# Moving operands of the Up and Down products: runs of 4 everywhere, weights 64 bytes off, another first matmul

## The chip, the cores and the metric

The kernel runs on one core of a Trainium2 chip. The metric is the device time of one execution in microseconds (us); the time before is the median of three executions, 1084.04 us (1083.44 to 1085.48). The engines have short names: PE is TensorE's matmul, PEld its loading of weights (of the stationary operand), DVE is VectorE, ACT is ScalarE, POOL is GpSimd, SP is SyncE, which issues the DMAs here.

## The reference

One layer of a hybrid decoder on 256 tokens with 2048 features, in float32. A combined input projection feeds two groups of heads, a state-space scan (SSD) and sparse attention; an output projection and a squared-ReLU MLP follow. By work it is nearly all four matrix products:

```python
h = rmsnorm(x, g_mix) @ w_in            # 256 x 2048 @ 2048 x 5728
...                                     # conv, SSD scan, index, top-k, attention
x = x + jnp.concatenate([y_ssd, y_att], axis=-1) @ w_out   # 2048 x 2048
u = rmsnorm(x, g_mlp) @ w_up            # 2048 x 8192
return x + jnp.square(jax.nn.relu(u)) @ w_down             # 8192 x 2048
```

## The kernel before

Precision comes from splitting. Each float32 operand is written as a rounded part hi and a rest lo (type float32r), and a product is hi·hi + hi·lo + lo·hi, three matmuls. `operands` (L119) brings in one piece of the weights by DMA into a tile `raw`, ScalarE casts it to hi (L135), VectorE subtracts to get lo (L136). Both lie in one tile `w2` of a ring of five, first hi, then lo, behind `shift` floats at the tile's start. Pieces are fetched ahead as buffers come free.

There are three forms of product. TensorE's instructions stand in the order in which the program is written; other tasks (attention, scan) are slipped in between by `step()`.

- `product` (L159) has tokens on partitions. The stationary operand is a 128 x 128 block of tokens (`hx`, `yah`/`yal`, `ysh`/`ysl`, `uh`/`ul`), the moving one a row of up to 512 weights. For each of 16 blocks kt along the contraction and each half b of the tokens it issues L173 (hi·hi), L175 (lo of the tokens, hi of the weights) and L176 (hi of the tokens, lo of the weights). It serves the input blocks k, m0 (304 columns), m1 (304), q0, q1, z0, z1, the output projection w_out (four blocks) and Down (four quarters q of four blocks, 384 matmuls in a quarter).
- `product_t` (L211) has features on partitions: the stationary operand is a block of weights, the moving one 256 tokens of `hx` (L224). It serves the input blocks qi and xbc.
- `product_w` (L231) is like it for the Up product, with hi and lo of the tokens side by side in `x2x`: a wide matmul of 512 columns (hi of the weights), then a narrow one of 256 (lo of the weights), both on L245. There are four quarters of 256 such pairs.

The order of the MLP is Up 0, Up 1, Down 0, Up 2, Down 1, Up 3, Down 2, Down 3.

The moving operand and the output are not streamed column by column from first to last. `walk` (L154) reorders them: with runs of 4 and steps of 16 it first takes columns 0 to 3, 16 to 19, 32 to 35 and so on to the end, then 4 to 7, 20 to 23, and so on, four sweeps in all. "Runs of 8" means 8 columns of every 32. `product_t` and the last Down block (`tail`) are not walked.

In the built program `hx`, `x2x`, `yah`, `yal`, `ysh`, `ysl`, `uh`, `ul` and all five `w2` buffers begin 96 bytes past a multiple of 128 in each partition, and slices within them are multiples of 128 bytes apart. So the distance between moving and stationary operand, modulo 128 bytes, is the shift: in `product` 8 floats (32 bytes) for the input blocks, w_out and Down 0 and 2, 24 floats (96 bytes) for Down 1 and the first three blocks of Down 3, 48 floats (192, that is 64 modulo 128) for the tail; in `product_t` 16 floats (64 bytes); in `product_w` 32 floats (128) for quarters 0 and 1 and none for quarters 2 and 3.

Where TensorE did something else just before a product, its first matmul is split in two: the list `other` collects what was issued, `interrupted` (L142) reads it. In `product` and `product_w` the first piece has 32 columns.

Of the kernel before, what the change touches and what calls it, by code (L numbers as in the profile page):

```python
# [18 lines left out]
T = 256  # L19
# [10 lines left out]
WB = 5  # L30
RB = 4

SPARE = 64
SHIFT = 16

QUADS, EIGHTS = (4, 16), (8, 32)
FIRST = 32
UP = [(QUADS, QUADS, 32), (QUADS, QUADS, 32), (EIGHTS, QUADS, 0), (EIGHTS, QUADS, 0)]  # L40
DOWN = [8, 24, 8, 24]


Z0, XBC0, DT0, Q0, K0, V0, QI0, KI0, WI0, END = (
# [31 lines left out]
def hymba_kernel(ctx: ExitStack, tc: tile.TileContext, xn, xt, w_in, w_out, w_up, w_down, vcol, vrow, out):  # L76
    nc = tc.nc
# [27 lines left out]
    def step():  # L105
        for t in list(tasks):
            if isinstance(t[1], int) and t[1] > 0:
                t[1] -= 1
            elif not isinstance(t[1], str) or t[1] in done:
                advance(t)  # L110
# [9 lines left out]
    def operands(src, n, load=None, shift=0, parts=2):  # L120

        pitch = (n + 63) // 64 * 64
        with tc.high_priority(offset=HP):
            raw = wts.tile([P, parts, pitch], F32, name="raw", tag="raw", bufs=RB)
            both = wts.tile([P, 2 * parts * pitch + SPARE], F32R, name="w2", tag="w2", bufs=WB)
            hi, lo = (both[:, shift + i * parts * pitch:shift + (i + 1) * parts * pitch]
                      .rearrange("p (k c) -> p k c", k=parts)[:, :, :n] for i in range(2))
            src = src.rearrange("p (k c) -> p k c", k=parts)
            step = parts if load is None else 1
            for i in range(0, parts, step):  # L130
                s = slice(i, i + step)
                nc.sync.dma_start(raw[:, s, :n], src[:, s])
                if load is not None:
                    load()
                nc.scalar.copy(hi[:, s], raw[:, s, :n])  # L135
                nc.vector.tensor_tensor(lo[:, s], raw[:, s, :n], hi[:, s].bitcast(F32), op=OP.subtract)  # L136
        return hi, lo
# [3 lines left out]
    def interrupted(kind):  # L141

        yes = any(o != kind for o in other)
        other.clear()
        return yes

    def mp(name):
        other.append(name)
        return ps.tile([P, 512], F32, name=name, tag="mid")

    def accumulator():
        return ps.tile([P, 512], F32, name="acc", tag="acc")

    def walk(a, way):  # L154

        run, step = way
        return a.rearrange("p (c k i) -> p k c i", k=step // run, i=run)

    def product(src, n, left, load=None, tail=None, shift=8):  # L159


        acc = [accumulator(), accumulator()]
        last = KT if tail is None else KT - 4

        def part(kt, out, b, wh, wl):
            s = slice(b * P, (b + 1) * P)
            ah, al = left(kt)
            free = tail is not None
            go = (lambda a: a) if free else (lambda a: walk(a, QUADS))

            at = [0, FIRST, n] if kt + b == 0 and interrupted("product") and not free else [0, out.shape[-1]]
            for i, j in zip(at, at[1:]):
                nc.tensor.matmul(go(out[:, i:j]), ah[:, s], go(wh[:, i:j]), start=(kt + i == 0), stop=False,  # L173
                                 skip_group_check=True)
            nc.tensor.matmul(go(out), al[:, s], go(wh), start=False, stop=False, skip_group_check=True)  # L175
            nc.tensor.matmul(go(out), ah[:, s], go(wl), start=False, stop=(kt == KT - 1), skip_group_check=True)  # L176

        kept = []
        halves = [slice(0, n // 2), slice(n // 2, n)]
        if tail is not None:  # L180
            acc.append(mp("acc_t"))
        for kt in range(KT):
            if kt % 2 == 0:
                hi, lo = operands(src[kt // 2], n, load, shift)
            wh, wl = hi[:, kt % 2], lo[:, kt % 2]
            if tail is None:
                for b in range(NB):
                    part(kt, acc[b][:, :n], b, wh, wl)
            elif kt < last:
                for c in halves if kt else [slice(0, n)]:  # L190
                    part(kt, acc[0][:, c], 0, wh[:, c], wl[:, c])
                for i, c in enumerate(halves):
                    part(kt, acc[1 + i][:, c], 1, wh[:, c], wl[:, c])
            else:
                kept.append((kt, wh, wl))
            step()
        if tail is not None:
            for kt, wh, wl in kept:
                for c in halves:
                    part(kt, acc[0][:, c], 0, wh[:, c], wl[:, c])  # L200
            tail(0, slice(0, n), acc[0])
            for i, c in enumerate(halves):
                for kt, wh, wl in kept:
                    part(kt, acc[1 + i][:, c], 1, wh[:, c], wl[:, c])
                tail(1, c, acc[1 + i][:, c])
        other.append("product")
        return acc

    def product_t(src, right):

        acc = accumulator().rearrange("p (c t) -> p c t", c=2)  # L211
        for i in range(4):
            hi, lo = operands(src[i], 1024, shift=SHIFT, parts=1)
            c = i % 2
# [13 lines left out]
        other.append("narrow")  # L228
        return acc

    def product_w(src, right, wide, narrow, shift):  # L231

        acc = [accumulator(), accumulator()]
        for i in range(4):
            hi, lo = operands(src[i], 1024, shift=shift, parts=1)
            out = acc[i % 2]
            for k in range(8):
                x = right(8 * (i // 2) + k)
                s = slice(k * P, (k + 1) * P)
                todo = [(hi, 0, 2 * T, wide), (lo, 0, T, narrow)]  # L240

                if interrupted("wide"):
                    todo[:1] = [(hi, 0, FIRST, wide), (hi, FIRST, 2 * T - FIRST, wide)]
                for j, (w, at, n, way) in enumerate(todo):
                    nc.tensor.matmul(walk(out[:, at:at + n], way), w[:, 0, s], walk(x[:, at:at + n], way),  # L245
                                     start=(i < 2 and k + j == 0), stop=(i >= 2 and k == 7 and j == len(todo) - 1),
                                     skip_group_check=True)
                if k % 4 == 3:
                    step()
        other.append("wide")  # L250
        return acc
# [47 lines left out]
    for name, cols in IN_BLOCKS:  # L299
        n = sum(b - a for a, b in cols)  # L300
# [3 lines left out]
    def in_block(name, load=None):  # L304
        o, n = in_off[name]
        src = w_in[o:o + n * D].rearrange("(g p c) -> g p c", g=8, p=P)
        return product(src, n, h_left, load)
# [434 lines left out]
    def run():  # L742
# [58 lines left out]
        for j in range(4):  # L801
            spawn(residual(j, product(w_out[j], 512, y_left)), f"res{j}")
# [4 lines left out]
    def x2(kt):  # L807
        if kt >= KT - 4:
            need("res3")
        return box[0][:, kt, :]  # L810

    first = product_w(w_up[0], x2, *UP[0])
    while tasks:
        step()
    sst = keep.tile([P, NB], F32, name="sst")
# [10 lines left out]
    def up(q):  # L826
        uh = mlp.tile([P, KT, T], F32R, name="uh")
        ul = mlp.tile([P, KT, T], F32R, name="ul")
        for j in range(8):
            r = mlp.tile([P, 2, T], F32, name="r")  # L830
            for c, acc in enumerate(first if q + j == 0 else product_w(w_up[8 * q + j], x2, *UP[q])):
                nc.scalar.copy(r[:, c], acc[:, T:])
                nc.vector.tensor_tensor(r[:, c], r[:, c], acc[:, :T], op=OP.add)  # L833
            nc.vector.scalar_tensor_tensor(r, r, 0.0, r, op0=OP.max, op1=OP.mult)
            s = slice(2 * j, 2 * j + 2)
            nc.scalar.copy(uh[:, s, :], r)
            nc.vector.tensor_tensor(ul[:, s, :], r, uh[:, s, :].bitcast(F32), op=OP.subtract)
        return uh, ul

    def down(q, u):  # L840
        for j in range(4):

            def add(b, c, acc):
                c = slice(512 * j + c.start, 512 * j + c.stop)
                nc.vector.scalar_tensor_tensor(xr[:, b, c], acc, rs4[:, b:b + 1], xr[:, b, c], op0=OP.mult, op1=OP.add)  # L845
                if q == 3:
                    nc.sync.dma_start(out[b * P:(b + 1) * P, c], xr[:, b, c])

            end = q == 3 and j == 3
            acc = product(w_down[4 * q + j], 512, lambda kt: (u[0][:, kt, :], u[1][:, kt, :]), tail=add if end else None, shift=48 if end else DOWN[q])  # L850
            for b in range(0 if end else NB):
                add(b, slice(0, 512), acc[b])

    u = [up(0)]
    for q in range(1, 4):
        u.append(up(q))
        down(q - 1, u[q - 1])
    down(3, u[3])


# [50 lines left out]
```

## Time and profile before

| | us |
|---|---|
| median of 3 executions | 1084.04 |
| profiled execution | 1085.21 |
| its span, first to last instruction | 1083.4 |
| TensorE busy | 1077.0 |
| weight loads busy | 946.2 |
| VectorE busy | 681.8 |
| ScalarE busy | 526.8 |

The profile is of one execution. Matmuls overlap in it: each is shown from its start to the end of its way through the array, and the next starts before that. The busy time of an engine counts overlapping time once. A row on a source line gives the shortest, middle and longest duration of its instructions and when the first and the last of them started.

### The profile page before, as it was taken

The page shows a single profiled execution, that of the slowest core. Times are in us where ns is not written, and L with a number is a line of the kernel's source. Part 1 is how long each engine was busy: PE and PEld are TensorE (multiplying, and loading weights), DVE is VectorE, ACT ScalarE, POOL GpSimd, SP SyncE. Part 2 cuts the span into 40 slices and gives each one's busy share as a digit, 9 for nine tenths or more (in the row PEclk, how much of TensorE's full clock was granted, in tenths as well). Part 3 has the DMA queues.
Part 4 walks back from the last instruction along what each step waited for, and adds up shares of the span by engine and source line. Part 5 has one row for each costly group of instructions (what it writes and reads, how often), then busy time and mean ns, then how long its engine had stood idle before and what let it go on. Part 6 is the DMA issues. An engine that isn't in the chain of part 4 may idle for free.

```text
span 1083.4 us, 15687 instructions
## 1 busy us (share of the span) xinstructions
PE 1077.0 (99%) x6086; PEld 946.2 (87%) x6086; DVE 681.8 (63%) x971; ACT 526.8 (49%) x725; POOL 24.4 (2%) x30
## 2 busy tenths in 40 slices
PE   9999999999999999999999999999999999999998
PEld 7999999888888888899888888888888888888888
DVE  6776899677765566666665556665455665555553
ACT  6755565556755454455543334444334444333331
POOL 0020000122000000000000000000000000000000
PEclk9999999999999999999999999999999999999999
DMA  9865446544375555555555555555555555555662
GB/s 303 278 214 176 156 127 199 184 148 136 120 269 179 191 191 198 195 195 196 198 198 194 197 195 193 197 199 188 186 192 194 195 194 195 194 194 195 214 214 77
DMA packets 64762, 207.41 MB, mean 191 GB/s; under 512 B 7216, under 2 KB 13616, under 8 KB 64688
## 3 DMA queue, kind: packets, MB, share of 16 engines
q1 hardware_dynamic: 64544, 206.36, 57.2%
q8 instruction: 48, 0.79, 0.3%
q14 instruction: 26, 0.21, 0.1%
q10 hardware_dynamic: 144, 0.05, 0.0%
HBM read 204.29 MB, written 2.10 MB: 190 GB/s over the span
## 4 chain that ended last, share of the span: by engine, by line
PE 95%; DMA 2%; DVE 2%; issue 1%; ACT 0%; SPq 0%; DVEq 0%; ACTq 0%
PE acc L245 32%; PE acc L173 16%; PE acc L176 16%; PE acc L175 16%; PE acc L224 9%; DMA raw<-in_w_in 2%; DVE w L136 1%; PE ps_y L622 1%; PE ps_sr L706 0%; PE ps_l L660 0%; PE ps_o L685 0%; DMA xT<-in_xt 0%; PE ps_s L512 0%; PE ps_s L513 0%; PE ps_dec L613 0%
## 5 line engine op out<-in xcount | busy, mean ns | idle before, releaser
L136 DVE TENSOR_TENSOR w<-raw,w 128x1024 fp32r<-128x1024 f32 (+3 forms) x400 | 466.5, 1169 | 370.9 <-ACT w L135 370.1
L135 ACT CAST w<-raw 128x1024 fp32r<-128x1024 f32 (+3 forms) x400 | 398.6, 999 | 496.2 <-PE acc L176 249.0
L245 PE MATMUL acc<-x2x,w 128*128 128x512 f32 (+2 forms) x2053 | 344.1, 328 | 0.0
L245 PEld LDWEIGHTS acc<-x2x,w 128*128 128x128 f32 x2053 | 308.2, 188 | 35.2
L173 PE MATMUL acc<-w,uh 128*128 128x512 f32 (+2 forms) x530 | 199.3, 377 | 0.0
L175 PE MATMUL acc<-w,ul 128*128 128x512 f32 (+1 forms) x527 | 199.0, 378 | 0.0
L176 PE MATMUL acc<-w,uh 128*128 128x512 f32 (+1 forms) x527 | 199.0, 378 | 0.0
L173 PEld LDWEIGHTS acc<-w,uh 128*128 128x128 f32 x530 | 99.0, 187 | 19.2
L176 PEld LDWEIGHTS acc<-w,uh 128*128 128x128 f32 x527 | 98.6, 187 | 19.1
L175 PEld LDWEIGHTS acc<-w,ul 128*128 128x128 f32 x527 | 98.6, 187 | 19.1
L224 PE MATMUL acc<-hx,w 128*128 128x256 f32 (+1 forms) x978 | 115.1, 277 | 0.0
L224 PEld LDWEIGHTS acc<-hx,w 128*128 128x128 f32 x978 | 112.8, 188 | 0.0
L173 PE MATMUL acc<-w,hx 128*128 128x512 f32 (+3 forms) x229 | 84.5, 372 | 0.4 <-ACT w L135 0.4
L176 PE MATMUL acc<-w,hx 128*128 128x512 f32 (+1 forms) x224 | 81.2, 362 | 0.1
L175 PE MATMUL acc<-w,hx 128*128 128x512 f32 (+1 forms) x224 | 81.0, 361 | 0.0
L173 PEld LDWEIGHTS acc<-w,hx 128*128 128x128 f32 x229 | 43.0, 189 | 6.9 <-ACT w L135 0.8
L176 PEld LDWEIGHTS acc<-w,hx 128*128 128x128 f32 x224 | 42.1, 188 | 6.9 <-DVE w L136 1.1
L175 PEld LDWEIGHTS acc<-w,hx 128*128 128x128 f32 x224 | 42.3, 189 | 6.4 <-issue 0.7
L845 DVE SCALAR_TENSOR_TENSOR xr<-acc,rs,xr 128x512 f32<-128x512 f32 (+1 forms) x32 | 22.3, 736 | 9.2 <-PE acc L176 9.2
L833 DVE TENSOR_TENSOR r<-r,acc 128x256 f32<-128x256 f32 x64 | 26.6, 416 | 0.0
L173 PE MATMUL acc<-w,yah 128*128 128x512 f32 (+2 forms) x68 | 25.7, 387 | 0.0
L175 PE MATMUL acc<-w,yal 128*128 128x512 f32 x64 | 24.7, 386 | 0.0
(215 smaller groups left out, 691.8 us busy)
## 6 DMA issues: line engine op xcount, KB each, us to landing
raw<-in_w_up SPq DMA_DIRECT2D x128, 512.0 KB, 3.3
raw<-in_w_down SPq DMA_DIRECT2D x128, 512.0 KB, 3.3
raw<-in_w_in SPq DMA_DIRECT2D x72, 512.0 KB, 3.5
raw<-in_w_out SPq DMA_DIRECT2D x32, 512.0 KB, 3.3
raw<-in_w_in SPq DMA_DIRECT2D x16, 256.0 KB, 4.3
raw<-in_w_in SPq DMA_DIRECT2D x16, 152.0 KB, 5.4
raw<-in_w_in SPq DMA_DIRECT2D x8, 304.0 KB, 3.2
xT<-in_xt SPq DMA_DIRECT2D x16, 128.0 KB, 4.4
```

What stands on the lines that cost most here:

```text
L135: nc.scalar.copy(hi[:, s], raw[:, s, :n])
L136: nc.vector.tensor_tensor(lo[:, s], raw[:, s, :n], hi[:, s].bitcast(F32), op=OP.subtract)
L173: nc.tensor.matmul(go(out[:, i:j]), ah[:, s], go(wh[:, i:j]), start=(kt + i == 0), stop=False, skip_group_check=True)
L175: nc.tensor.matmul(go(out), al[:, s], go(wh), start=False, stop=False, skip_group_check=True)
L176: nc.tensor.matmul(go(out), ah[:, s], go(wl), start=False, stop=(kt == KT - 1), skip_group_check=True)
L224: nc.tensor.matmul(acc[:, c, at:at + n], w[:, 0, s], x[:, fr:fr + n], start=(i + k + j == 0), stop=(i >= 2 and k == 7 and j == len(todo) - ...
L245: nc.tensor.matmul(walk(out[:, at:at + n], way), w[:, 0, s], walk(x[:, at:at + n], way), start=(i < 2 and k + j == 0), stop=(i >= 2 and k ...
L622: nc.tensor.matmul(pt[:, 64 * i:64 * i + 64], m[i // 4][:, i % 4, :], xdt[:, c, 64 * h:64 * h + 64], start=True, stop=True)
L833: nc.vector.tensor_tensor(r[:, c], r[:, c], acc[:, :T], op=OP.add)
L845: nc.vector.scalar_tensor_tensor(xr[:, b, c], acc, rs4[:, b:b + 1], xr[:, b, c], op0=OP.mult, op1=OP.add)
```

## The change

Four things change. `product_w` takes runs of 4 and steps of 16 for both matmuls and a shift of 32 floats in all quarters, where quarters 2 and 3 had runs of 8 of 32 in the wide matmul and no shift. `product` shifts its weights by 16 floats (64 bytes) everywhere but in the tail, which stays at 48. The split first matmul of `product` has 320 and 192 columns instead of 32 and 480, and blocks of 304 columns (m1) are not split. `product_w` keeps 32 and 480. All start addresses but the weights' stay as they are.

```diff
-QUADS, EIGHTS = (4, 16), (8, 32)
-FIRST = 32
-UP = [(QUADS, QUADS, 32), (QUADS, QUADS, 32), (EIGHTS, QUADS, 0), (EIGHTS, QUADS, 0)]
-DOWN = [8, 24, 8, 24]
+SHIFT_W = 32
+
+RUN = 4
+STEP = 16
+
+FIRST = 320
+FIRST_W = 32
...
-    def walk(a, way):
-
-        run, step = way
-        return a.rearrange("p (c k i) -> p k c i", k=step // run, i=run)
-
-    def product(src, n, left, load=None, tail=None, shift=8):
+    def walk(a):
+
+        return a.rearrange("p (c k i) -> p k c i", k=STEP // RUN, i=RUN)
+
+    def product(src, n, left, load=None, tail=None):
...
-            go = (lambda a: a) if free else (lambda a: walk(a, QUADS))
-
-            at = [0, FIRST, n] if kt + b == 0 and interrupted("product") and not free else [0, out.shape[-1]]
+            go = (lambda a: a) if free else (lambda a: walk(a))
+
+            at = [0, FIRST, n] if kt + b == 0 and interrupted("product") and n == 512 and not free else [0, out.shape[-1]]
...
-                hi, lo = operands(src[kt // 2], n, load, shift)
+                hi, lo = operands(src[kt // 2], n, load, SHIFT if tail is None else SPARE - SHIFT)
...
-    def product_w(src, right, wide, narrow, shift):
+    def product_w(src, right):
...
-            hi, lo = operands(src[i], 1024, shift=shift, parts=1)
+            hi, lo = operands(src[i], 1024, shift=SHIFT_W, parts=1)
...
-                todo = [(hi, 0, 2 * T, wide), (lo, 0, T, narrow)]
+                todo = [(hi, 0, 2 * T), (lo, 0, T)]

                 if interrupted("wide"):
-                    todo[:1] = [(hi, 0, FIRST, wide), (hi, FIRST, 2 * T - FIRST, wide)]
+                    todo[:1] = [(hi, 0, FIRST_W), (hi, FIRST_W, 2 * T - FIRST_W)]
...
-            acc = product(w_down[4 * q + j], 512, lambda kt: (u[0][:, kt, :], u[1][:, kt, :]), tail=add if end else None, shift=48 if end else DOWN[q])
+            acc = product(w_down[4 * q + j], 512, lambda kt: (u[0][:, kt, :], u[1][:, kt, :]), tail=add if end else None)
```

On TensorE, at the place where Down 0 follows Up 1, stands this before (a row is line, operation, output and operands, shape; 4x2x4 is four sweeps of two runs of 4, thus 32 columns):

```order
L245 MATMUL acc<-x2x,w_5549 128x4x32x4
L245 MATMUL acc<-x2x,w_5549 128x4x16x4
L173 MATMUL acc<-w_5579,uh 128x4x2x4
L173 MATMUL acc<-w_5579,uh 128x4x30x4
L175 MATMUL acc<-w_5579,ul 128x4x32x4
```

And this now, at the same place:

```order
L245 MATMUL acc<-x2x,w_5548 128x4x32x4
L245 MATMUL acc<-x2x,w_5548 128x4x16x4
L173 MATMUL acc<-w_5578,uh 128x4x20x4
L173 MATMUL acc<-w_5578,uh 128x4x12x4
L175 MATMUL acc<-w_5578,ul 128x4x32x4
```

The first L173 grows from 32 to 320 columns and the second shrinks from 480 to 192; nothing else moves. The next place is on TensorE too, where Up 2 follows Down 0. Before (4x16x8 is four sweeps of sixteen runs of 8):

```order
L176 MATMUL acc<-w_6119,uh 128x4x32x4
L245 MATMUL acc<-x2x,w_6143 128x32
L245 MATMUL acc<-x2x,w_6143 128x4x15x8
L245 MATMUL acc<-x2x,w_6143 128x4x16x4
L245 MATMUL acc<-x2x,w_6143 128x4x16x8
L245 MATMUL acc<-x2x,w_6143 128x4x16x4
```

And now:

```order
L176 MATMUL acc<-w_6118,uh 128x4x32x4
L245 MATMUL acc<-x2x,w_6142 128x4x2x4
L245 MATMUL acc<-x2x,w_6142 128x4x30x4
L245 MATMUL acc<-x2x,w_6142 128x4x16x4
L245 MATMUL acc<-x2x,w_6142 128x4x32x4
L245 MATMUL acc<-x2x,w_6142 128x4x16x4
```

The number and the sizes of the instructions stay; the wide ones are walked in runs of 4. The shift of the weights shows in no row, since rows carry no addresses. The whole program has one matmul less, at the start of m1.

## Rows read from the trace of the kernel before

**Rows 1.** The page's engine table and clock by fortieths of the span.
```profile
PE 1077.0 (99%) x6086; PEld 946.2 (87%) x6086; DVE 681.8 (63%) x971; ACT 526.8 (49%) x725; POOL 24.4 (2%) x30
...
PEclk9999999999999999999999999999999999999999
```
**Rows 2.** The page's chain of work that ended last, by engine and line.
```profile
PE 95%; DMA 2%; DVE 2%; issue 1%; ACT 0%; SPq 0%; DVEq 0%; ACTq 0%
PE acc L245 32%; PE acc L173 16%; PE acc L176 16%; PE acc L175 16%; PE acc L224 9%; DMA raw<-in_w_in 2%; DVE w L136 1%; PE ps_y L622 1%; PE ps_sr L706 0%; PE ps_l L660 0%; PE ps_o L685 0%; DMA xT<-in_xt 0%; PE ps_s L512 0%; PE ps_s L513 0%; PE ps_dec L613 0%
```
**Rows 3.** Waits of PE: waited for, us in total, times, longest us.
```profile
PE ps_w L260 <- POOL ones L255: 1.3, 1, 1.3
PE ps_ki L438 <- DVE kd L433: 1.2, 1, 1.2
PE acc L173 <- ACT w L135: 0.4, 1, 0.4
```
**Rows 4.** Windows: length; busy PE, PEld, DVE, ACT, POOL; clock; DMA share, GB/s.
```profile
0.00:27.00 27.00, 25.73 (x108) 21.16 (x109) 18.13 (x40) 18.62 (x39) 1.29 (x10) 1.00 0.92 302
27.00:54.00 27.00, 26.36 (x201) 25.37 (x199) 19.94 (x76) 21.44 (x51) 0.00 (x0) 1.00 0.82 281
...
558.80:645.50 86.70, 86.70 (x389) 72.00 (x387) 45.31 (x43) 34.33 (x34) 0.00 (x0) 1.00 0.58 194
731.50:820.60 89.10, 89.10 (x389) 72.06 (x387) 45.34 (x43) 34.31 (x34) 0.00 (x0) 1.00 0.56 189
```
**Rows 5.** L175, Down 0 to 3: count, duration min/median/max ns, first and last start.
```profile
L175 PE MATMUL acc<-w,ul x128: 380/385/393, 559.2 to 645.0; 128*128 128x512 f32 x128
L175 PE MATMUL acc<-w,ul x128: 380/392/397, 731.9 to 820.1; 128*128 128x512 f32 x128
L175 PE MATMUL acc<-w,ul x128: 380/385/393, 906.9 to 992.8; 128*128 128x512 f32 x128
L175 PE MATMUL acc<-w,ul x96: 383/386/391, 993.4 to 1057.6; 128*128 128x512 f32 x96
```
**Rows 6.** L175 in three stretches: w_out late, w_out middle, m1.
```profile
L175 PE MATMUL acc<-w,ysl x16: 381/381/381, 376.6 to 386.5; 128*128 128x512 f32 x16
L175 PE MATMUL acc<-w,yal x4: 397/397/397, 343.3 to 345.4; 128*128 128x512 f32 x4
L175 PE MATMUL acc<-w,hx x22: 294/294/294, 168.1 to 176.5; 128*128 128x304 f32 x22
```
**Rows 7.** L224 of `product_t`, 81 to 99 us; L175 in Down 3's tail.
```profile
L224 PE MATMUL acc<-hx,w x161: 276/276/276, 80.8 to 98.9; 128*128 128x256 f32 x161
L175 PE MATMUL acc<-w,ul x30: 276/276/276, 1060.9 to 1073.8; 128*128 128x256 f32 x30
```
**Rows 8.** L245 of Up quarters 1, 2 and 3, wide and narrow together.
```profile
L245 PE MATMUL acc<-x2x,w x509: 271/382/382, 473.8 to 558.5; 128*128 128x512 f32 x85, 128*128 128x256 f32 x85
L245 PE MATMUL acc<-x2x,w x508: 272/331/404, 645.8 to 730.9; 128*128 128x256 f32 x85, 128*128 128x512 f32 x85
L245 PE MATMUL acc<-x2x,w x509: 272/380/460, 820.6 to 905.9; 128*128 128x256 f32 x85, 128*128 128x512 f32 x84, 128*128 128x480 f32 x1
```
**Rows 9.** Lines by form, 181 to 297 and 297 to 387 us: busy, mean ns.
```profile
L175 PE MATMUL acc<-w,hx 128*128 128x512 f32 x128 | 49.2, 384 | 0.0
...
L175 PE MATMUL acc<-w,yal 128*128 128x512 f32 x64 | 24.7, 386 | 0.0
...
L175 PE MATMUL acc<-w,ysl 128*128 128x512 f32 x64 | 24.5, 382 | 0.0
```
**Rows 10.** Timeline where Down 0 begins: start us, length us, count; loads, then matmuls.
```profile
558.71 0.30 PEld L173 LDWEIGHTS acc<-w,uh 128*128 128x128 f32 x2
558.93 0.19 PEld L175 LDWEIGHTS acc<-w,ul 128*128 128x128 f32 x1
...
558.82 0.49 PE L173 MATMUL acc<-w,uh 128*128 128x32 f32 x2
559.15 0.38 PE L175 MATMUL acc<-w,ul 128*128 128x512 f32 x1
```

More of the change, by code (lines that the diff above doesn't have):

```diff
@@ L239, in product_w @@
                 s = slice(k * P, (k + 1) * P)
-                todo = [(hi, 0, 2 * T, wide), (lo, 0, T, narrow)]
+                todo = [(hi, 0, 2 * T), (lo, 0, T)]
                 if interrupted("wide"):
-                    todo[:1] = [(hi, 0, FIRST, wide), (hi, FIRST, 2 * T - FIRST, wide)]
-                for j, (w, at, n, way) in enumerate(todo):
-                    nc.tensor.matmul(walk(out[:, at:at + n], way), w[:, 0, s], walk(x[:, at:at + n], way),
+                    todo[:1] = [(hi, 0, FIRST_W), (hi, FIRST_W, 2 * T - FIRST_W)]
+                for j, (w, at, n) in enumerate(todo):
+                    nc.tensor.matmul(walk(out[:, at:at + n]), w[:, 0, s], walk(x[:, at:at + n]),
                                      start=(i < 2 and k + j == 0), stop=(i >= 2 and k == 7 and j == len(todo) - 1),
@@ L810, in x2 @@
         return box[0][:, kt, :]
-    first = product_w(w_up[0], x2, *UP[0])
+    first = product_w(w_up[0], x2)
     while tasks:
@@ L830, in up @@
             r = mlp.tile([P, 2, T], F32, name="r")
-            for c, acc in enumerate(first if q + j == 0 else product_w(w_up[8 * q + j], x2, *UP[q])):
+            for c, acc in enumerate(first if q + j == 0 else product_w(w_up[8 * q + j], x2)):
                 nc.scalar.copy(r[:, c], acc[:, T:])
```

## The prediction

> **What bounds the kernel now.** I read the engine table first. TensorE is busy for 1077.0 of 1083.4 us, at the full granted clock in every slice [rows 1]. The chain of waits agrees: 95% of it is TensorE, and the lines named are the three of `product` (L173, L175, L176), `product_w` (L245) and `product_t` (L224) [rows 2]. Third, the waits: TensorE sat idle behind another engine for under 3 us in all [rows 3]. So the reader has to ask how often a matmul starts, not what it waits for. A matmul's own duration is no help with that, because consecutive matmuls overlap. I take the distance between starts: in a row of a line's instructions, (last start - first start) / (count - 1), and for L175, which is every third matmul of `product`, a third of that. I call this the pitch.
>
> The fourth view gives the pitch of the same 512-column matmul in the four quarters of the Down product [rows 5]: 225.2 ns (85.8 us over 127 x 3), 231.5 (88.2), 225.5 (85.9) and 225.3 (64.2 over 95 x 3). Nothing differs between quarters 0 and 1 but the weights' shift, 8 against 24 floats. VectorE and ScalarE do the same work in both (45.3 and 34.3 us) and DMA is at 0.58 and 0.56, yet one takes 86.70 us and the other 89.10 [rows 4]. Quarter 3 has the same shift as quarter 1 and is 6 ns faster; it starts directly behind another Down product, quarter 1 behind an Up product and a split matmul. So the pitch depends on where the moving operand lies against the stationary tokens, and on how the run was entered. The lowest pitch of a 512-column matmul in any settled stretch is 220.0 ns (9.9 us over 15 x 3, in w_out), and there every duration is the same 381 ns [rows 6]. The highest is some 233 (2.1 us over 3 x 3), where all take 397.
>
> Now by distance. All token and weight tiles start at the same residue of 128 bytes, so the shift in bytes is the distance between moving and stationary operand:
> - 64 bytes, unwalked, 256 columns (`product_t`): 113.1 ns (18.1 us over 160), all durations 276; the tail of the last Down product, also 64 bytes and unwalked, has 276 throughout as well [rows 7].
> - 0 modulo 128, runs of 4 (Up quarter 1): 333.5 ns for a pair of 512 and 256 columns (84.7 us over 508, doubled) [rows 8]. That is 220.0 + 113.1 and 0.4 over.
> - 0, runs of 8 for the wide one (Up quarters 2 and 3): 335.7 and 335.8 [rows 8].
> - 32 bytes, runs of 4: 220.0 in some stretches, 225 in others, 233 for a short one; 304 columns 133.3 (8.4 us over 21 x 3) [rows 5, 6].
> - 96 bytes, runs of 4: 231.5 or 225.3 [rows 5].
>
> So where the distance is a multiple of 64 and the walk is of 4 or none, every stretch lies at the lowest level seen; at 32 and 96 there are several levels.
>
> **The change part by part.** The profiled execution took 1085.2 us (span 1083.4 and 1.8 around it), 1.2 above the median of 1084.0; I take the savings off its own stages and the sum off the median.
>
> *Up quarters 2 and 3.* They get the walk and shift of quarter 1, with the same x2x tile and the same five buffers. 335.7 less 333.5 is 2.2 ns for each of 2 x 256 pairs: 1.1 us less. Between 0, were the buffers' order in time to matter, and 1.1: quarter 1 is at the lowest level already. Its wide matmul behind a Down product keeps its split of 32 and 480.
>
> *Products with tokens on partitions: 64 bytes.* The trace has no walked product at 64 bytes. From below, 220.0 ns bounds it: no settled stretch is under it, so I exclude a further gain. From above, 233. I take 220.0, since the row nearest in distance (`product_t`, 64 bytes) and the row nearest in walk at a multiple of 64 (Up quarter 1) both lie at the floor. Down then gives (225.2 - 220) x 384 + (231.5 - 220) x 384 + (225.5 - 220) x 384 + (225.3 - 220) x 288 = 2.0 + 4.4 + 2.1 + 1.5 = 10.0 us. For the input blocks q0 to z1 and w_out I use durations, since stalls of other origin stand between their starts: L175 has a mean of 384, 386 and 382 ns against 381 at the floor [rows 9], so 3 ns x 384 + 3 ns x 384 = 2.3 us. The blocks k and m0 I count at nothing: the DMA engines are at 0.92 and 0.82 there [rows 4], so an earlier TensorE would wait for weights. Elsewhere they stand near 0.6, and weights are prepared five buffers ahead. If that cover failed it would show as L173 waiting for the casts, 0.4 us now [rows 3].
>
> *First matmul of 320 and 192 columns.* With 32 and 480 the next matmul starts 0.33 us after the first (559.15 less 558.82) instead of 0.22, because three weight loads go through at 0.11 us each (558.71 to 558.93 for two) and the 480 columns start their stream only behind the second [rows 10]. With 320 the stream takes 133.3 ns for 304 columns and 7 more, 140, which hides the second load; the 192 that follow can't be shorter than the next load's 110. So 0.25 us and 0.08 saved, in 11 places (four input blocks, four of w_out, three of Down); `m1` loses its split altogether, 0.1. Together 1.0 us; between 0 and 1.0, zero being that two split matmuls again cost what the present two do. The tail of the last product keeps its 48 floats and its order.
>
> Sum: 1.1 + 10.0 + 2.3 + 0.9 (the split, with a little off for the few matmuls until a run has settled) = 14.3 us less; 1084.0 - 14.3 = 1069.7, and I say 1070.
>
> The Trainium skill, "TensorE: Matmul & The Clock Gate", Part 2 (step 1, LDWEIGHTS), says that TensorE has two independent read ports into SBUF, and that loading the next weights takes no bandwidth from the running matmul. Under this rule the distance could not matter and 64 bytes would be worth nothing; quarters 0 and 1 of Down, 86.70 against 89.10 us, disagree with it as far as addresses explain them. It is the third rival.
>
> **The rivals.**
> 1. *A middle level.* Walked at 64 bytes, a run locks where Down quarters 0, 2 and 3 are now, at 225.2. Quarter 1 gains (231.5 - 225.2) x 384 = 2.4 us; input blocks and w_out lose the stretches that are at 220 today: (225.2 - 220) x 768 - 2.3 = 1.7. With Up and the splits: -1.1 - 0.9 - 2.4 + 1.7 = -2.7, 1081.3. For it: the same instructions at 32 bytes show 220 and 225 side by side, so a place has more than one level. Against it: no stretch at a multiple of 64 shows a second one with runs of 4.
> 2. *Slower: it locks high.* One place, the settled walked run; one price, 231.5 ns as in Down quarter 1. Quarters 0 and 2 lose 6.3 and 6.0 x 384, quarter 3 6.2 x 288, together 6.5 us; input blocks and w_out 11.5 x 768 - 2.3 = 6.5; less 2.0 for Up and splits: +11.0, 1095. At 233 it is some 1098. It decides where the mean pitch of the 2208 walked matmuls passes today's 225.6 ((12.3 us over the floor) / 2208) by more than 2.0 us / 2208 = 0.9, so at 226.5 ns. For it: 24 floats did this beside an Up product. Against: that distance is no multiple of 64.
> 3. *The distance does nothing*, and the levels are set only by how a run is entered: with Down as it is, and Up unchanged as well, the splits alone are left: 1083.
> 4. *Part of the runs settle low.* A new beginning of 320 and 192 may put some runs at the floor and leave others at 225; half of the 12.3 us: 1084.0 - 2.0 - 6.2 = 1075.8.
>
> **How the numbers follow.** The forecast 0.60; rival 4 0.15; rival 1 0.07; rival 3 0.04; rival 2 0.14. Its own range is 1067.5 (a full 1.0 for the splits, and k and m0 giving something after all) to 1073. The range asked for reaches over rivals 4 and 1 to 1082.5, and leaves out the slow rival, most of rival 3 and a little below: 0.2. About 2.2 us (0.2%) is what a measurement can tell from no change. Faster by more: the forecast, rival 4 and nearly all of rival 1, 0.80. Within: rival 3 and the rest of 1, 0.06. Slower: 0.14.
>
> **What would show it.** Right: L175 in all four Down quarters with one duration near 381 ns and a pitch of 220; quarters 0 to 2 each about 84.7 us long instead of 86.7, 89.1 and 86.6; L245 at 333.5 ns for a pair in all quarters; 0.25 us from a Down product's first matmul to its L175. Wrong: durations of L175 that alternate among three or more values, with a pitch of 225 or above, in the stretches without a wait; Up quarters 2 and 3 still at 86.0 us; or the time saved coming back as waits of L173 for the casts, which the idle column would show.

## The result and the profile after

The changed kernel takes 1077.43 us (median of 4 executions, 1077.06 to 1077.68), the kernel before 1084.76 beside it (4 executions, 1083.44 to 1087.48). The ratio is 0.9929, with a 95% interval of 0.9909 to 0.9949: faster by 0.5 to 0.9%. The forecast was 1070.0 with 1067.5 to 1082.5: sign and range held, and half of the gain was missing.

The profiled executions compare by their spans, 1083.4 and 1075.5 us: 7.9 less. First the page's engine table after, and its shares of the chain by engine.

```profile
PE 1068.8 (99%) x6085; PEld 946.3 (88%) x6085; DVE 681.4 (63%) x971; ACT 526.8 (49%) x725; POOL 24.2 (2%) x30
...
PE 95%; DVE 2%; DMA 1%; ACT 1%; issue 1%; SPq 0%; ACTq 0%; DVEq 0%
```

Against [rows 1, 2] TensorE's busy time fell by 8.2 us with the work of the other engines unchanged, and the chain is TensorE's as before. The waits after are as small as in [rows 3]; the casts that a faster TensorE might have had to wait for cost it 1.0 us.

```profile
PE ps_w L260 <- POOL ones L255: 1.3, 1, 1.3
PE acc L173 <- ACT w L136: 1.0, 1, 1.0
PE ps_ki L438 <- DVE kd L433: 0.9, 1, 0.9
```

So the time lies in the pitch again. Windows of the kernel after from the start of m1 on, columns as in [rows 4]: m1; the input blocks q0 to z1; w_out; Down 0; Up 2; Down 1; Up 3; Down 2; Down 3 up to its tail.

```profile
165.60:180.20 14.60, 14.60 (x109) 14.60 (x108) 14.36 (x34) 8.60 (x13) 0.00 (x0) 1.00 0.60 197
180.20:295.20 115.00, 115.00 (x578) 97.32 (x578) 83.31 (x137) 69.48 (x115) 16.47 (x12) 1.00 0.47 156
295.20:385.40 90.20, 90.20 (x425) 76.14 (x424) 54.19 (x72) 48.04 (x69) 0.00 (x0) 1.00 0.63 210
...
557.40:643.20 85.80, 85.80 (x387) 72.04 (x386) 45.22 (x43) 34.30 (x34) 0.00 (x0) 1.00 0.59 197
643.20:728.70 85.50, 85.50 (x515) 76.94 (x514) 54.25 (x63) 41.24 (x54) 0.00 (x0) 1.00 0.59 197
728.70:814.50 85.80, 85.80 (x389) 72.00 (x387) 45.20 (x43) 34.30 (x34) 0.00 (x0) 1.00 0.58 196
814.50:899.90 85.40, 85.40 (x514) 76.85 (x513) 54.11 (x63) 41.22 (x54) 0.00 (x0) 1.00 0.61 197
899.90:985.70 85.80, 85.80 (x387) 72.03 (x386) 45.19 (x43) 34.30 (x34) 0.00 (x0) 1.00 0.60 196
985.70:1050.00 64.30, 64.30 (x289) 53.94 (x288) 33.36 (x31) 25.13 (x24) 0.00 (x0) 1.00 0.66 213
```

The clock is 1.00 in all of them. The lengths before are the windows between the same first matmuls.

| stage | before, us | after, us | difference | forecast |
|---|---|---|---|---|
| up to m1 | 167.1 | 165.6 | -1.5 | 0 |
| m1 | 14.0 | 14.6 | +0.6 | -0.1 |
| q0 to z1, with the attention | 115.5 | 115.0 | -0.5 | -2.9 |
| w_out | 90.3 | 90.2 | -0.1 | (in the row above) |
| Up 0 and 1 | 171.9 | 172.0 | +0.1 | 0 |
| Up 2 and 3 | 172.0 | 170.9 | -1.1 | -1.1 |
| Down 0 to 2 | 262.4 | 257.4 | -5.0 | -8.7 |
| Down 3 to its tail | 64.8 | 64.3 | -0.5 | -1.5 |
| tail | 25.4 | 25.5 | +0.1 | 0 |

The Down products bring 5.5 of the 7.9 us. Their L175 after, quarters 0 to 3, as in [rows 5]:

```profile
L175 PE MATMUL acc<-w,ul x128: 382/385/407, 557.7 to 642.8; 128*128 128x512 f32 x128
...
L175 PE MATMUL acc<-w,ul x126: 382/384/385, 730.3 to 814.0; 128*128 128x512 f32 x126
...
L175 PE MATMUL acc<-w,ul x126: 382/384/385, 901.5 to 985.3; 128*128 128x512 f32 x126
...
L175 PE MATMUL acc<-w,ul x96: 382/384/385, 986.0 to 1049.6; 128*128 128x512 f32 x96
```

85.1 us over 127 x 3, 83.7 and 83.8 over 125 x 3 and 63.6 over 95 x 3 are pitches of 223.4, 223.2, 223.5 and 223.2 ns: one level for four runs that had 225.2, 231.5, 225.5 and 225.3, and not the 220.0 that I took. The durations tell the same without arithmetic: a run at the lowest level has one duration, 380 or 381 ns; these have 382 and 385 in turn (the median of 384 shown lies between). The lowest level is in this kernel too, at the same distance and with the same walk, in block k and at the beginning of w_out:

```profile
L175 PE MATMUL acc<-w,hx x28: 380/380/380, 9.8 to 27.6; 128*128 128x512 f32 x28
...
L175 PE MATMUL acc<-w,yal x15: 380/380/380, 297.0 to 306.2; 128*128 128x512 f32 x15
...
L175 PE MATMUL acc<-w,ysl x16: 382/384/385, 374.9 to 385.0; 128*128 128x512 f32 x16
...
L175 PE MATMUL acc<-w,hx x28: 300/303/303, 165.8 to 177.1; 128*128 128x304 f32 x28
```

The second row is 9.2 us over 14 x 3, 219.0 by these rounded starts; the third, late in w_out where [rows 6] has 381 throughout, is 10.1 over 15 x 3, 224. The last row is m1, which settled with 303 ns and a pitch of 140 (11.3 over 27 x 3 gives 139.5), where it had 294 and 133.3.

Up 2 has (728.3 - 643.2) / 511 x 2 = 333.1 ns a pair, as Up 1 in [rows 8], and Up 3 (814.5 to 899.6 us) the same; the median of 330 lies between the narrow and the wide form:

```profile
L245 PE MATMUL acc<-x2x,w x512: 177/330/463, 643.2 to 728.3; 128*128 128x512 f32 x85, 128*128 128x256 f32 x85, 128*128 128x32 f32 x1
```

Where Down 0 begins, the timeline shows the new split, against [rows 10] (loads left out; x2 is both pieces):

```profile
557.43 0.39 PE L173 MATMUL acc<-w,uh 128*128 128x320 f32 x2
...
557.66 0.41 PE L175 MATMUL acc<-w,ul 128*128 128x512 f32 x1
...
557.91 0.39 PE L176 MATMUL acc<-w,uh 128*128 128x512 f32 x1
```

From the first piece to L175 it takes 0.23 us instead of 0.33; the next start follows 0.25 later instead of 0.22. So 0.07 us is left of each split.

### The profile page after: what moved, and what is told of

It reads as the page before. It is cut to its first block, busy times and chain, and to the rows that moved or that the text cites. A ratio compares the mean times of both kernels' runs of the same rounds, so it can differ in the third digit from the quotient of the medians.

```text
span 1075.5 us, 15686 instructions
## 1 busy us (share of the span) xinstructions
PE 1068.8 (99%) x6085; PEld 946.3 (88%) x6085; DVE 681.4 (63%) x971; ACT 526.8 (49%) x725; POOL 24.2 (2%) x30
## 4 chain that ended last, share of the span: by engine, by line
PE 95%; DVE 2%; DMA 1%; ACT 1%; issue 1%; SPq 0%; ACTq 0%; DVEq 0%
PE acc L245 32%; PE acc L175 16%; PE acc L176 16%; PE acc L173 16%; PE acc L224 9%; DVE w L137 1%; PE ps_y L622 1%; DMA xrow<-in_xn 1%; ACT w L136 1%; PE ps_sr L706 0%; PE ps_l L660 0%; PE ps_o L685 0%; DMA xT<-in_xt 0%; DMA raw<-in_w_in 0%; PE ps_s L512 0%
## 5 line engine op out<-in xcount | busy, mean ns | idle before, releaser
L245 PE MATMUL acc<-x2x,w 128*128 128x512 f32 (+2 forms) x2053 | 343.0, 327 | 0.0
L245 PEld LDWEIGHTS acc<-x2x,w 128*128 128x128 f32 x2053 | 308.0, 188 | 34.3
L175 PE MATMUL acc<-w,ul 128*128 128x512 f32 (+1 forms) x527 | 197.3, 374 | 0.0
L173 PE MATMUL acc<-w,uh 128*128 128x512 f32 (+2 forms) x530 | 197.2, 373 | 0.0
L224 PE MATMUL acc<-hx,w 128*128 128x256 f32 (+1 forms) x978 | 115.3, 278 | 0.0
L173 PEld LDWEIGHTS acc<-w,uh 128*128 128x128 f32 x530 | 99.1, 187 | 17.4
L175 PEld LDWEIGHTS acc<-w,ul 128*128 128x128 f32 x527 | 98.7, 187 | 17.4
L224 PEld LDWEIGHTS acc<-hx,w 128*128 128x128 f32 x978 | 113.0, 188 | 0.0
L173 PE MATMUL acc<-w,hx 128*128 128x512 f32 (+3 forms) x228 | 83.5, 369 | 1.0 <-ACT w L136 1.0
L175 PE MATMUL acc<-w,hx 128*128 128x512 f32 (+1 forms) x224 | 80.7, 360 | 0.0
L173 PEld LDWEIGHTS acc<-w,hx 128*128 128x128 f32 x228 | 42.9, 189 | 7.2 <-ACT w L136 1.4
L175 PEld LDWEIGHTS acc<-w,hx 128*128 128x128 f32 x224 | 42.1, 188 | 5.7 <-issue 0.7
L173 PE MATMUL acc<-w,yah 128*128 128x512 f32 (+2 forms) x68 | 25.3, 381 | 0.0
L173 PE MATMUL acc<-w,ysh 128*128 128x512 f32 x64 | 24.7, 386 | 0.0
```

The costliest lines, as they stand in the source:

```text
L224: nc.tensor.matmul(acc[:, c, at:at + n], w[:, 0, s], x[:, fr:fr + n], start=(i + k + j == 0), stop=(i >= 2 and k == 7 and j == len(todo) - ...
L245: nc.tensor.matmul(walk(out[:, at:at + n]), w[:, 0, s], walk(x[:, at:at + n]), start=(i < 2 and k + j == 0), stop=(i >= 2 and k == 7 and j ...
```

## The experiments

The question is why runs of 4 at 64 bytes stood at 223.3 ns in Down and at 220.0 elsewhere. Three theories went into the experiments. **A**: a run falls into a repeating cycle of starts, and which one depends on distance, walk, and the state in which it is entered, the split among it. **B**: distance and walk alone set the level. **C**: the level is that of whatever ran ahead, and only a gap of some 300 ns or more sets a run free. Pitches below are worked out from the rows as above; single times are of one profiled execution each. The kernel before, run once beside them, took 1087.72 us beside the first four kernels, 1088.48 beside the next four and 1085.46 beside the two of "What a run inherits"; the single times are therefore no measure of a gain, and the argument goes by the stages.

**Up alone.** The kernel before with

```diff
-UP = [(QUADS, QUADS, 32), (QUADS, QUADS, 32), (EIGHTS, QUADS, 0), (EIGHTS, QUADS, 0)]
+UP = [(QUADS, QUADS, 32)] * 4
```

> The kernel before with the Up part alone: all quarters in runs of 4 with a shift of 32 floats; the products with tokens on partitions as before. Theory A (level set by distance, walk and how the run is entered) and theory B (level set by distance and walk alone) both expect Up 2 and 3 at 333.4 ns for a pair instead of 335.7 (L245, 85.4 us a quarter instead of 86.0), so 1.1 us less. A also allows Down 1 to enter at another level (225 instead of 231.5), since what runs ahead of it is another; B does not.

It took 1082.40 us. Up 2, then Down 1:

```profile
L245 PE MATMUL acc<-x2x,w x512: 177/330/463, 643.8 to 729.0; 128*128 128x512 f32 x85, 128*128 128x256 f32 x85, 128*128 128x32 f32 x1
...
L175 PE MATMUL acc<-w,ul x128: 380/392/396, 729.6 to 817.9; 128*128 128x512 f32 x128
```

A pair takes 333.5 ns in Up 2 and 333.1 in Up 3, and Down 1 stays at 231.5 (88.3 over 381). Up's gain is its own, and Down 1's high level does not come from the walk of Up 2 ahead of it. In this run m1 began at 165.4 us, with the code of before up to there, which began it at 167.1; the 1.5 us that the changed kernel has before m1 are within such scatter.

The same pair of executions shows that the program alone doesn't fix a level. Up to Up 2 the two programs are one and the same. In one stretch of `product_t` (64 bytes, not walked, 256 columns) before, then here:

```profile
L224 PE MATMUL acc<-hx,w x52: 276/276/282, 56.6 to 62.4; 128*128 128x256 f32 x52
...
L224 PE MATMUL acc<-hx,w x51: 281/281/281, 54.8 to 60.6; 128*128 128x256 f32 x51
```

That is 113.7 and 116.0 ns by these rounded starts, 113.3 and 117.8 by the unrounded ones. The stretch begins behind a pause (1.44 us before, 1.04 here), and its first starts, read unrounded, are 326, 85, 142 and 113 ns apart before, 325, 85, 145 and 109 here. So one distance, walk and split can settle at two levels, and what differs ahead of them is the pause and a few ns in the entry.

**The new shifts with the old split, and the old shifts with the new split.** The first is the changed kernel with

```diff
-FIRST = 320
+FIRST = 32
...
-            at = [0, FIRST, n] if kt + b == 0 and interrupted("product") and n == 512 and not free else [0, out.shape[-1]]
+            at = [0, FIRST, n] if kt + b == 0 and interrupted("product") and not free else [0, out.shape[-1]]
```

> The changed kernel with the first matmul split into 32 and 480 again, m1 split too (32 and 272). Theory A: the pitch of the settled Down runs moves between the two levels that 64 bytes has, 220.0 and 223.3 ns, in at least one quarter, and m1 leaves 140 ns for 133.3; theory B: Down stays at 223.3 and m1 at 140. Either way each of eleven entries costs 0.08 us more (0.33 instead of 0.25 from first matmul to L175), 0.9 us.

It took 1080.30 us. Down 0 to 3, and Up 3, which follows Down 1:

```profile
L175 PE MATMUL acc<-w,ul x128: 378/383/388, 560.7 to 645.5; 128*128 128x512 f32 x128
...
L175 PE MATMUL acc<-w,ul x128: 382/384/388, 731.8 to 816.9; 128*128 128x512 f32 x128
...
L175 PE MATMUL acc<-w,ul x128: 380/380/386, 905.4 to 989.2; 128*128 128x512 f32 x128
...
L175 PE MATMUL acc<-w,ul x96: 380/380/380, 989.9 to 1052.6; 128*128 128x512 f32 x96
...
L245 PE MATMUL acc<-x2x,w x512: 178/333/469, 817.3 to 904.7; 128*128 128x512 f32 x85, 128*128 128x256 f32 x85, 128*128 128x32 f32 x1
```

Down stands at 222.6, 223.4, 220.0 and 220.0: three levels from the same distance, walk and split, so B falls. Down 2 and 3 are lower than in the changed kernel, and Up 3 is higher, 342.1 ns a pair, 2.3 us over the quarter. The second is the kernel before with

```diff
-            at = [0, FIRST, n] if kt + b == 0 and interrupted("product") and not free else [0, out.shape[-1]]
+            at = [0, 320, n] if kt + b == 0 and interrupted("product") and n == 512 and not free else [0, out.shape[-1]]
```

> The kernel before with the split of 320 and 192 alone (m1 not split), shifts of 8 and 24 floats and Up as they were. Theory A: at least one of Down 0 to 2 leaves its level of 225.2, 231.5 or 225.5 ns. Theory B: all three stay, and only the 0.08 us at each entry is saved, 0.9 us in all.

It took 1080.97 us. Down 0 to 2:

```profile
L175 PE MATMUL acc<-w,ul x128: 381/381/413, 557.1 to 641.0; 128*128 128x512 f32 x128
...
L175 PE MATMUL acc<-w,ul x128: 382/392/410, 727.7 to 815.9; 128*128 128x512 f32 x128
...
L175 PE MATMUL acc<-w,ul x128: 380/385/410, 902.6 to 988.5; 128*128 128x512 f32 x128
```

220.2, 231.5 and 225.5. At 32 bytes the new split, here and in the products ahead, takes Down 0 from 225.2 to the floor, and leaves Down 2, at the same distance, where it was. Down 1 at 96 bytes keeps 231.5 with either split. So both halves of the change move levels, and they don't add: the shifts alone bring Down (2.6 + 8.1 + 5.5) x 384 + 5.3 x 288 = 7.7 us, more than the 5.3 that its pitch brings with the new split.

**Other splits at 64 bytes.** Three kernels give each Down quarter a split of its own (quarter 3 runs on from quarter 2), with m1 split after 32, 160 and 272:

```diff
+FIRST_DOWN = [(), (32,), (64,), ()]
...
+            acc = product(w_down[4 * q + j], 512, lambda kt: (u[0][:, kt, :], u[1][:, kt, :]), tail=add if end else None, first=FIRST_DOWN[q])
```

> The changed kernel with another first matmul in each Down quarter: none split in Down 0, 32 columns in Down 1, 64 in Down 2; m1 split at 32. Theory A: not all three settle at 223.3 ns, and each entry that leads to 220.0 saves 1.3 us in a quarter (384 x 3.3 ns), 2.2 us where Down 3 follows. Theory B: all four quarters stay at 223.3 and m1 at 140.

```diff
+FIRST_DOWN = [(128,), (192,), (256,), ()]
```

> The changed kernel with a first matmul of 128 columns in Down 0, 192 in Down 1, 256 in Down 2, m1 split at 160. Theory A (the state in which a run is entered chooses among the levels that its distance has): at least one of these quarters is not at 223.3 ns; each at 220.0 saves 1.3 us, 2.2 where Down 3 follows. Theory C (only a gap of 300 ns or more in which TensorE starts nothing sets a run free, the place of the split does not): the quarters stay at 223.3.

```diff
+FIRST_DOWN = [(384,), (448,), (480,), ()]
```

> The same with 384, 448 and 480 columns first in Down 0, 1 and 2, m1 split at 272. A second piece of 128 columns or fewer is shorter than the load behind it, 0.11 us. Theory A: at least one quarter away from 223.3 ns, up to 2.2 us less or, at the level of 341.98 ns a pair that Up 3 showed when Down 1 had begun with 32 columns, 2.2 us more in an Up quarter. Theory C: 223.3 throughout.

They took 1081.18, 1076.03 and 1079.33 us. Down 0 to 2 of the second:

```profile
L177 PE MATMUL acc<-w,ul x128: 380/380/388, 557.4 to 641.2; 128*128 128x512 f32 x128
...
L177 PE MATMUL acc<-w,ul x128: 382/385/389, 727.4 to 812.5; 128*128 128x512 f32 x128
...
L177 PE MATMUL acc<-w,ul x128: 378/383/388, 898.6 to 983.4; 128*128 128x512 f32 x128
```

128 columns in Down 0 give 220.0 (83.8 over 381), 192 in Down 1 223.4, 256 in Down 2 222.6. Without a split, with 32 and with 64, all three quarters took 223.4 to 223.6; with 384 in Down 0 220.5 and a single duration of 380 ns for most, with 448 and 480 223.4 and 223.6. A's expectation for the first kernel, that not all three settle at 223.3, missed; that kernel by itself agrees with B, and it is 128, 256 and 384 columns that don't. Up 3 was at 342 ns a pair behind a Down 1 that began with 32 or 448.

**Other walks and other distances.** The changed kernel, Down's quarters walked otherwise:

```diff
+WAYS = [None, (8, 32), (4, 8), (4, 8)]
...
-            go = (lambda a: a) if free else (lambda a: walk(a))
+            go = (lambda a: a) if free or way is None else (lambda a: walk(a, way))
```

> The changed kernel with other orders of the columns in Down, all at 64 bytes: not walked in Down 0, runs of 8 of 32 in Down 1, runs of 4 of 8 in Down 2 and 3. If the levels come from moving and weight reads meeting in SBUF, each order has its own set of levels: the unwalked one should lie at 220.0 ns as product_t and the tail do at the same distance (113.3 for 256 columns), or at 225 as product_t did for one stretch of the changed kernel; the others are open, between 220 and 235. If order has no part in it, all stay at 223.3.

It took 1089.76 us. Down 0 (not walked), 1 (8 of 32) and 2 (4 of 8):

```profile
L176 PE MATMUL acc<-w,ul x128: 394/394/417, 560.1 to 647.3; 128*128 128x512 f32 x128
...
L176 PE MATMUL acc<-w,ul x128: 394/394/412, 733.5 to 819.8; 128*128 128x512 f32 x128
...
L176 PE MATMUL acc<-w,ul x128: 393/394/417, 906.0 to 994.9; 128*128 128x512 f32 x128
```

228.9, 226.5 and 233.3 ns: at 64 bytes, too, the unwalked matmul of 512 columns isn't at the floor. The row of `product_t` in [rows 7], unwalked at the same distance, was one of my two nearest rows and didn't carry over; it has another width and other operands, and no run shows which of the two matters. Down 0 is the clean comparison, since nothing ahead of it was changed: 228.9 against 223.4 ns by the order of the columns. Down 0 and 1 repeat one duration, 394 ns, and still are not at the floor. Then the weights' shift in floats for each quarter (0, 16, 48 and 128 bytes):

```diff
+SHIFT_DOWN = [0, 4, 12, 32]
```

> The changed kernel with runs of 4 and other shifts in Down: 0 floats in Down 0, 4 (16 bytes) in Down 1, 12 (48 bytes) in Down 2, 32 (128 bytes, thus 0) in Down 3 up to the tail. Theory A with distance: Down 0 and Down 3 share one set of levels, 16 and 48 bytes have others, between 220 and 235 ns. If distance has no part in it: 223.3 in all.

It took 1082.44 us. Down 0 to 3:

```profile
L176 PE MATMUL acc<-w,ul x128: 379/384/417, 557.7 to 642.8; 128*128 128x512 f32 x128
...
L176 PE MATMUL acc<-w,ul x128: 380/388/407, 728.9 to 815.8; 128*128 128x512 f32 x128
...
L176 PE MATMUL acc<-w,ul x128: 382/387/412, 901.9 to 987.7; 128*128 128x512 f32 x128
...
L176 PE MATMUL acc<-w,ul x93: 387/394/394, 990.4 to 1053.9; 128*128 128x512 f32 x93
```

223.4, 228.1, 225.2 and (63.5 over 92 x 3) 230.1. Nothing ahead of Down 0 was changed; its pitch is that of the changed kernel, but its durations take four values from 379 to 390 ns (379, 382, 385 and 390) where they had 382 and 385. Down 1 has the same instructions, split and engine work in this kernel and in the changed one, and 228.1 against 223.2 ns; as Down 0 ahead of it has another shift too, its own shift is not proved to be the cause. Distance 0 shows two levels, 223.4 in Down 0 and 230.1 in Down 3, where 128 bytes is the same distance by my measure; I can't say whether the predecessor or the absolute address made that difference.

**What a run inherits.** Two kernels repeat splits in other quarters, with m1 at 32 bytes and split after 32, and at 64 and split after 64:

```diff
+FIRST_DOWN = [(128,), (128,), (384,), ()]
```

> The changed kernel with 128 columns first in Down 0 and 1, 384 in Down 2, and m1 back at 8 floats with a split of 32. Theory A, with the state that an Up quarter leaves behind counting too: Down 0 at 220.0 ns again, as with 128 before; Down 1 and 2 are entered behind an Up quarter at 333.1 a pair, and with 320 they ran through the same starts, so they answer alike to a value: 128 and 384 tell two values; each that leads to 220.0 saves 1.3 us (Down 1) or 2.2 (Down 2 and 3). m1 at 133.8 instead of 140: 0.6 less. If the state before counted for nothing, 128 and 384 would give 220.0 in all, as in Down 0.

```diff
+FIRST_DOWN = [(128,), (96,), (160,), ()]
```

> The same with 96 columns first in Down 1, 160 in Down 2, m1 at 64 bytes with a split of 64. Down 0 at 220.0 by theory A, as it is entered as in the run with 128. Down 1 and 2 are open: 220.0, 222.7 or 223.3; the level of Up 3 too, 333.1 or 342.0 ns a pair.

They took 1081.62 and 1083.74 us. Down 1 and 2 of the first, then Down 2 of the second:

```profile
L177 PE MATMUL acc<-w,ul x128: 380/380/380, 730.4 to 814.2; 128*128 128x512 f32 x128
...
L177 PE MATMUL acc<-w,ul x128: 382/390/441, 900.3 to 987.4; 128*128 128x512 f32 x128
```

```profile
L177 PE MATMUL acc<-w,ul x128: 389/397/398, 900.0 to 988.9; 128*128 128x512 f32 x128
```

128 gives 220.0 again, in Down 0 and 1. But 384 columns, which put Down 0 at 220.5, put Down 2 at 228.6, and 160 put it at 233.3, above anything that Down had before: the end that I had given the slow rival is real at this very distance and walk. The two runs that begin with 384 columns stand behind the same kind of Up product and begin nearly alike (L175 to L177 0.23 and 0.22 us, the next start 0.28 in both); what differs is what lies further back, a few ns in the first starts, and which of the five buffers comes first. I take the state to be inherited across the Up product; no run here shows what it consists of, nor that the buffers have no part in it.

m1 tells shift and split apart, since up to there the kernels held against each other differ in m1's shift or split alone. Before, and in the first kernel here, 32 bytes and a split of 32 give 133.3 ns (9.6 us over 24 x 3). Below are 32 bytes unsplit (the kernel before with the new split), 64 bytes with a split of 32 and 64 bytes with a split of 272 (the first and the third kernel of "Other splits at 64 bytes"):

```profile
L175 PE MATMUL acc<-w,hx x24: 293/298/306, 168.1 to 177.5; 128*128 128x304 f32 x24
...
L177 PE MATMUL acc<-w,hx x24: 292/300/310, 168.3 to 177.9; 128*128 128x304 f32 x24
...
L177 PE MATMUL acc<-w,hx x24: 295/295/295, 168.6 to 178.0; 128*128 128x304 f32 x24
```

These are 136.2, 139.1 and 136.2 ns (9.4, 9.6 and 9.4 over 23 x 3); 64 bytes unsplit is the 140 of the changed kernel. With the split of 32 kept, the shift alone takes m1 from 133.3 to 139; with the shift kept, dropping the split takes it to 136. Either alone raises it. A stretch of `product_t` had two levels in two executions, but m1 repeats: all four kernels with 32 bytes and a split of 32 have 133.3, all four with 64 bytes unsplit have 140, both with 64 bytes and a split of 32 have 139; the other splits were run once each. The return to 133.3 that A expected for a split of 32 at 64 bytes didn't come.

**128 columns everywhere, and the best of each stage.** The changed kernel with `FIRST = 128`, and one that has besides w_out at its old 32 bytes with 320 and m1 as it was before:

```diff
-FIRST = 320
+FIRST = 128
```

> The changed kernel with one number changed: 128 columns first in place of 320 in all products that are split. Theory A: Down at 220.0 ns throughout, if the state that the input blocks and w_out leave behind is lost in Up 0, as it was in every run so far: 4.8 us less than 1077.4, 1072.6, give or take 1 for w_out and the input blocks, whose levels are drawn anew at each entry. Otherwise Down 0 leaves 220.0 and with it the later quarters may.

```diff
+        return product(src, n, h_left, load, None, *((32, 8) if name == "m1" else ()))
...
+            spawn(residual(j, product(w_out[j], 512, y_left, shift=8)), f"res{j}")
...
+            acc = product(w_down[4 * q + j], 512, lambda kt: (u[0][:, kt, :], u[1][:, kt, :]), tail=add if end else None, first=128)
```

> The changed kernel with 128 columns first in all Down quarters, w_out back at a shift of 8 floats (with 320 and 192), m1 at 8 floats with a split of 32. Theory A with the inherited state: Down 2 is entered like Down 1, so all of Down lies at 220.0 ns: 1440 x 3.3 ns = 4.8 us less than the changed kernel; w_out near 221.4 instead of 223.5 ns, 0.8 less; m1 133.8 instead of 140, 0.6 less: some 1071.2 us by the median of the changed kernel, 1077.4. If the levels of single stretches don't carry over when stages are combined, Down 2 and 3 lie at 223 to 233 and the time is between 1073 and 1090.

With 128 everywhere it took 1073.54 us (1072.39 to 1074.28, 4 executions), 0.9900 of the kernel before (0.9884 to 0.9917); the mixed one 1071.80 (1071.59 to 1073.18, 4), 0.9887 (0.9872 to 0.9901). The two intervals overlap. Both beat the changed kernel: the upper ends lie at 1074.28 and 1073.18, its lowest at 1077.06, though not in the same sitting (the kernel before had 1084.34 in that of the two and 1084.76 in that of the changed kernel). Down 0 and Down 3 of the mixed one (Down 1 and 2 have 380 ns throughout as well):

```profile
L175 PE MATMUL acc<-w,ul x128: 380/380/387, 556.7 to 640.6; 128*128 128x512 f32 x128
...
L175 PE MATMUL acc<-w,ul x96: 380/380/380, 981.2 to 1043.9; 128*128 128x512 f32 x96
```

Its windows of m1, w_out and Down 0:

```profile
165.90:179.90 14.00, 14.00 (x109) 14.00 (x108) 13.76 (x33) 7.45 (x11) 0.00 (x0) 1.00 0.61 187
295.60:384.50 88.90, 88.90 (x422) 75.36 (x421) 53.95 (x72) 47.32 (x68) 0.00 (x0) 1.00 0.64 213
556.50:641.00 84.50, 84.50 (x387) 72.12 (x386) 45.09 (x43) 34.26 (x34) 0.00 (x0) 1.00 0.61 200
```

Each of Down 0 to 2 takes 84.5 us, below the 84.7 that I had forecast for the floor. DMA stays at 0.61 and no wait came in the floor's place: only the level had been missing. All ten Down quarters that began with 128 columns at 64 bytes, in five kernels, settled at 220.0. That is a finding on Down, not on 128: in the kernel with 128 everywhere the four blocks of w_out, at 64 bytes too, have durations of 382 to 385 ns for the most part and settle at 223.2 to 223.5 ns between starts.

## Why the prediction was right and where it failed

- **What bounds it: right.** No wait appeared and the other engines' work is the same; every difference beyond the scatter before m1 is one of pitch.
- **Up, 1.1 us: right.** 1.1 in the changed kernel; the same level with Up alone.
- **Down, 10.0 us: mis-sized, 5.3 by pitch.** The step that failed is "I take 220.0, since the row nearest in distance and the row nearest in walk at a multiple of 64 both lie at the floor". Each row stood for one property with another size or product, and the sentence behind it, that every stretch at a multiple of 64 lies at the lowest level, was an average over few runs with few entries: the nearest row in distance, `product_t`, has a second level itself, 117.8 instead of 113.3 ns, in another execution of the same program up to there. Runs of 4 at 64 bytes have at least five levels: 220.0, 222.6, 223.4, 228.6 and 233.3. The new split happened to enter the third, in all quarters; no row that I had told which. That it wasn't the fifth is luck: at 233.3 Down alone would have lost 8.1, 1.8 and 7.8 x 384 and 8.0 x 288 ns, 9.1 us.
- **Input blocks and w_out, 2.3 us: failed by the same step.** With the eight splits 0.6 us came of 2.9. In w_out L175 has means of 385 and 384 ns where it had 386 and 382 [rows 9]: one half lower, one higher. w_out takes 1.3 us less (88.9) at 32 bytes with the 320 split.
- **The splits, 0.08 us each: right in size** (0.07), but their cost is small beside what they decide: 128 for 320 is worth 3.9 us by the medians of the two sittings.
- **m1, 0.1 us gain: wrong sign.** It lost 0.6 us. I gave it the split's price and no level of its own. At 32 bytes it stands at 133.3 ns with its split and 136 without; at 64 bytes at 136 (split of 272), 139 (32) or 140 (unsplit). Shift and missing split both raised it.
- **The rivals.** Rival 4 came nearest in time (1075.8), but not as it happened: Down's runs weren't divided between two levels. Rival 1, a middle level for all walked runs, is nearest in mechanism, with another size: with 223.3 in place of 225.2 its sum is -1.1 - 0.9 - 5.3 + (3.3 x 768 - 2.3 = 0.2) = -7.1, thus 1076.9 against 1077.43 measured. My argument against it was the one that failed. Rival 2 didn't occur here, but 160 columns show that its price was fair. Rival 3 falls: with everything ahead and the split of 32 the same, m1 moves from 133.3 to 139 ns by its shift alone. The rule of the Trainium skill that I weighed there ("TensorE: Matmul & The Clock Gate", Part 2, step 1: two independent read ports, loading the next weights takes no bandwidth from the running matmul) leaves, as I read it, no room for an influence of the distance between the operands. These runs move the weights' address, and with it the distance, so they refute my reading that the address is of no account. They don't show the rule itself to be wrong: that it is the loads that get in the way was only argued, since no run took the loads away or moved both operands together.
- **C falls too:** a split of 128 columns brings Down to 220.0 with starts 57 and 226 ns apart at its beginning, so without a gap of 300 ns, and so does 384 in Down 0. Of A the core stands, that the entry chooses among several cycles, and that what lies further back has a part in it is likely but not shown by itself; A foretells no level for an untried split.

## What to carry to other kernels

Where a stage is bound by the rate at which matmuls start, compare pitches of the same instruction between stretches before anything else: equal work at unequal pitch is time to be had. A single repeated duration is no proof of the lowest level (394 ns repeated at 226.5 and 228.9, 281 in `product_t` at 117.8); the pitch decides. Treat a level as settled only for the product, width, distance, walk and entry in which it was seen, and price an untried combination with all levels that any of its kin have shown. The size of the first matmul of a run is a cheap knob; try several in each place, since the best in one place may be among the worst in another.

## What the runs showed of the hardware

- One walk, one distance and one split gave 220.5 and 228.6 ns (384 columns, Down 0 and Down 2), with the same kind of product ahead. If the past is what tells them apart, it outlives an Up product of 85 us.
- `product_t` (256 columns, one weight load each) ran at 113.3 ns in one execution and at 117.8 in another, at the same place of the same program; their first starts differed by at most 4 ns.
- Up with runs of 4 has a second level too, 342.1 instead of 333.1 ns a pair, seen only in Up 3 behind a Down 1 at 64 bytes that began with 32 or 448 columns; behind a Down 1 at 96 bytes that began with 32 it had 333.1.
- At 64 bytes and a split of 320, Down 0 takes 223.4 ns in runs of 4 of 16 and 228.9 in plain order. Runs of 8 of 32 gave 226.5 and of 4 of 8 233.3, each behind other quarters and in one entry; runs of 4 of 16 have themselves shown 220.0 to 233.3 at this distance, so the two are no measure of the order alone.
- No settled stretch in any kernel was below 220.0 ns for 512 columns. What sets that floor, and what the cycles are made of, stays open.
